# A two-block network on one Trainium2 core: where the last gates, a norm, the state tables and a square root stand

## The chip, the cores and the metric

One core of a Trainium2 chip runs the whole program. Its engines work side by side, each through its own list of instructions in order: TensorE (PE; its weight loads are listed apart, as PEld), VectorE (DVE), ScalarE (ACT), GpSimd (POOL) and SyncE (SP), which here only starts DMA transfers. They wait for one another through semaphores. The metric is the time of one execution in microseconds (us); less is better.

## The reference

Input and output are 512 tokens of width 1024, in 32-bit floats.

```python
def first_block(x, ...):
    h = rms_norm(x, g_mix)
    u, gb, gc, q, k, v = split(h @ w_in)
    y_conv = gb * short_conv(gc * u, conv_w)           # causal, width 3, 512 columns
    y_attn = dilated_mixture(q, k, v)                  # 8 heads, three dilated windows
    mix = concat(rms_norm(y_conv, g_conv_out), rms_norm(y_attn, g_attn_out))
    x = x + mix @ w_out
    h = rms_norm(x, g_ffn)
    return x + (silu(h @ w_gate) * (h @ w_up)) @ w_down

def second_block(x, c, ...):
    shift, scale, gate = split(silu(c) @ w_mod + b_mod)
    h = rms_norm(x) * (1 + scale) + shift
    xa, za, q, k, v, zb, qi, ki, wi, ga, gb = split(h @ w_in)
    ya = gelu(s5_mixer(xa, ...))                       # state space model, 32 groups of 16, state 64
    g = ya @ w_glu + b_glu
    ya = (g[:, :512] * sigmoid(g[:, 512:]) * silu(za)) @ w_a_o
    yb = (dsa_mixer(q, k, v, qi, ki, wi) * silu(zb)) @ w_b_o   # attention over 128 selected keys
    x = x + gate * ((sigmoid(ga) * ya + sigmoid(gb) * yb) @ w_out)
    return rms_norm(x) * final_g
```

## The kernel before

**Layout.** Activations lie transposed, features on partitions and 512 tokens along the free side. Weights stream through a ring of three buffers; ScalarE rounds each to a high part `wh` (L97), VectorE makes the rest `wl` (L98), and each product is three matmuls of 128x512 (`mm3`, L193 to L195). A 128-column step of a projection over 1024 features is 24 such matmuls.

**Order.** PE's order is the order in which the code is written. The lists of the other engines are made by a scheduler, which pulls ahead what is written under `high_priority`. Both attentions are loops over 32 steps (4 blocks of queries by 8 heads): a score, its softmax (L258 to L265: minimum, exponential, reciprocal, scaling), three steps later the transposes (L306), later the products with the values (L283). Between them the loop calls a *filler* for a set number of steps, so that PE has projections while a softmax runs.

**The first attention** has `conv()` as its filler, and after it `mix_out(ch, sqc)`, the convolution's half of the output projection. Eight blocks `n` of 128 columns are summed; after block 0 comes the norm (`rms`, which issues L219 on PE and then `rms_of`: L225, L228 and the 12 operations of `rsqrt` on VectorE, L204 to L212: a guess from the bits and three Newton steps), and after block 2 `spread` (L236) brings the 4x128 roots to all partitions through PE. `cl3` is the low part of the last convolution channel (L504). `mix_out(yh, sqa)` does the same for the attention's half.

**The feed-forward part** has `ssm_tables` beside it, a generator that is advanced a step at a time. After setting up exponentials, sines (on POOL, `pi`, `pr`) and coefficients, it makes for each of four chunks `c` of 8 groups three tables in DRAM: `tabs[2]` from `ca`, `tabs[0]` from `bts` (PE transposes of `ba`, L933, copied by ScalarE, L934), and `tabs[1]` from `tt`, the direct terms: a block of zeros in SBUF into which eight DMAs lay shifted pieces of `kk`, and which a ninth stores. `bts` and `tt` share one buffer (tag `io`).

**The second attention** has `gates()` as its filler: eight projections with a SiLU, then `tanhs(range(6))`, six of eight projections whose tanh opens the merge, and then `chunk_out(c)` for c of 0 to 3, with one more projection after chunks 0 and 1. A chunk copies 64 states into `hs` (POOL, L1199), loads `cat` (L1202) and `tt` (L1204) from the tables, and issues eight pairs of matmuls, L1208 and L1209. `cat` and `tt` of all chunks go through two buffers in all, so a chunk's loads start when the chunk before has been multiplied.

**The end.** The output projection is followed by the last norm, in two halves of 256 tokens: `norm(0)` among the last products, `norm(1)` behind them. Each is sum (L1386), `rms_of`, `spread` (L236), product, store.

Of the kernel before, what the change touches and what calls it, by code (L numbers as in the profile page):

```python
# [9 lines left out]
F = mybir.dt.float32  # L10
# [8 lines left out]
S = 512  # L19
# [9 lines left out]
RAW = 3  # L29
WARM = 8  # L30
FILLA = (3.0, 4.0, 5.0, 2.6)
# [3 lines left out]
class K:  # L35
# [185 lines left out]

    def rms_of(self, pool, p, n, tag, room=None):
        toks = p.shape[1] // P
        d = pool.tile([P, 4, P], F, name="spd")[:, :toks]
        self.V.tensor_mul(d, p.rearrange("p (i t) -> p i t", t=P),  # L225
                          self.ident[:, None, :].to_broadcast([P, toks, P]))
        s = pool.tile([P, 4], F, name=tag + "s")[:, :toks]
        self.V.tensor_reduce(s, d, axis=AX.X, op=OP.add)  # L228
        return self.rsqrt(pool, s, 1.0 / n, EPS, tag, room)

# [85 lines left out]
    def mixer(self):  # L316
# [179 lines left out]
        def conv():  # L496
# [43 lines left out]
            for _ in range(3):  # L540
                yield
            yield from mix_out(ch, sqc)

        def mix_out(ys, sq):

            pend = []
            for n in range(8):
                if n % 2 == 0:
                    wh, wl = self.w()
                p = self.acc()  # L550
                cs = slice(n % 2 * P, n % 2 * P + P)
                yield from self.steps(p, (wh[:, :, cs], wl[:, :, cs]), ys)
                with self.tc.high_priority(offset=LEAD):
                    if n == 0:
                        r = self.rms(sm, [sq], 512, "rx")
                    if n == 2:
                        Rn = self.spread(sm, r, sm.tile([P, S], F, name="Rx"))
# [20 lines left out]
        self.drain()  # L578
        self.run(mix_out(yh, sqa))
        cst.close()  # L580
# [4 lines left out]
    def ffn(self, x1):  # L585
# [10 lines left out]
        tabs = ExitStack()  # L596
        table = self.ssm_tables(tabs)
        for _ in range(2):
# [221 lines left out]

    def ssm_tables(self, st):
        nc, a, V, A, G, T = self.nc, self.a, self.V, self.A, self.G, self.T
# [51 lines left out]
        yield  # L874
        nr = p.tile([P, 48], F, name="snr")
        V.tensor_scalar(nr, pr[:, 1], -1.0, None, op0=OP.add)
# [27 lines left out]
        yield  # L904
        self.tabs = self.dram.tile([3, 4, P, S * 2], F, name="tabs")
        for c in range(4):
            gs = slice(8 * c, 8 * c + 8)
            def table(x, y, nj, name):
# [17 lines left out]
                                ca[:, :, 1:].rearrange("p g j x -> p g (j x)"))  # L926
            bts = p.tile([P, 8, P], F, name="bts", tag="io")
            kk = p.tile([16, 8, P], F, name="kk")
# [20 lines left out]
            V.tensor_add(kk[:, :, 0:16], kk[:, :, 0:16], de)  # L949
            tt = p.tile([P, 8, P], F, name="tt", tag="io")  # L950
            G.memset(tt, 0.0)
            for j in range(8):
                s = 7 - j
                nc.sync.dma_start(tt[16 * j:16 * j + 16, :, 16 * s:], kk[:, :, 0:P - 16 * s])
            nc.sync.dma_start(self.tabs[1, c], tt.rearrange("p g x -> p (g x)"))

# [57 lines left out]
    def hybrid(self, xs, second, close, out):  # L1014
# [222 lines left out]
        def gates():  # L1237
# [8 lines left out]

            yield from tanhs(range(6))
            for _ in cin:
# [3 lines left out]
            for c in range(4):  # L1252
                yield from chunk_out(sso, c)
                yield from tanhs(range(6 + c, min(7 + c, 8)))

# [77 lines left out]
        for m in range(4):  # L1333
# [6 lines left out]
            for e in range(2):  # L1340
# [6 lines left out]
                mg.append((hi, lo))  # L1347
        sq = x3p.tile([P, S], F, name="sqE")
        ws = [self.w() for _ in range(2)]
        ps = [self.acc() for _ in range(2)]  # L1350
# [27 lines left out]
        def norm(e):  # L1378
# [6 lines left out]
            with self.tc.high_priority(offset=200):  # L1385
                T.matmul(p, self.ones, sqs[e][3], start=False, stop=True)  # L1386
                r = self.rms_of(x3p, p, D, "re")
            for k in range(8):
# [15 lines left out]
        self.run(last(5, 1))  # L1404
        self.pad(x3p, 352)
        first, second = norm(0), norm(1)
# [110 lines left out]
```

## Time and profile before

| what | value |
|---|---|
| three runs, us | 1020.39, 1019.31, 1023.4 (median 1020.39) |
| profiled execution, us | 1019.43 |
| its span in the trace, us | 1017.6 |
| PE busy, us (share of the span) | 992.5 (98%) |
| DVE busy, us | 687.6 (68%) |
| ACT busy, us | 420.7 (41%) |
| POOL busy, us | 145.2 (14%) |
| mean granted clock of TensorE, share of full speed | 0.994 |

The span is the time from the first to the last instruction of the trace; the profiled execution's own time is 1.83 us longer. The two clocks of TensorE's matmuls are 2.4 GHz (a granted clock of 1.00) and 1.2 GHz (0.50). Lines are those of the kernel before; in the changed kernel the same code stands 15 lines lower behind `rms_of`, and up to 31 lower towards the end.

### The profile page before, as it was taken

To read this page: it belongs to the slowest core of one execution; us is meant where nothing else is said; L and a number is where in the kernel's file an instruction comes from. 1 tells how busy PE (TensorE), PEld (TensorE's weight loads), DVE (VectorE), ACT (ScalarE), POOL (GpSimd) and SP (SyncE) were. 2 spreads that over 40 slices of the span, in tenths; PEclk is the share of its full clock that TensorE was granted. 3 is DMA by queue.
4 is the path that set the end of the run, shared out by engine and by line. 5 is a ranking of instruction groups with operands and counts; after the bars stand their busy time and mean duration, and the time that the engine had idled before them with its cause. 6 is when DMAs were issued, how large, how long until landed. Compare 5 with 4: busy or idle time off the path is not lost.

```text
span 1017.6 us, 13862 instructions
## 1 busy us (share of the span) xinstructions
PE 992.5 (98%) x5074; PEld 824.4 (81%) x5074; DVE 687.6 (68%) x1334; ACT 420.7 (41%) x710; POOL 145.2 (14%) x324
## 2 busy tenths in 40 slices
PE   9999999999999999999999999999999979999995
PEld 7888887887777778888888898788888878888885
DVE  6886778786997847787653238599995555544444
ACT  6455556443333333233222225556445553333251
POOL 0000000007711100000010100001888130000020
PEclk9999999999999999999999999999999999999998
DMA  7343221223245576465552323343222352343212
GB/s 268 98 135 104 79 84 42 63 89 127 67 142 171 142 219 213 144 203 185 169 170 90 114 93 129 121 133 112 89 83 104 109 160 63 116 173 104 83 42 83
DMA packets 56100, 125.12 MB, mean 123 GB/s; under 512 B 17824, under 2 KB 24480, under 8 KB 55904
## 3 DMA queue, kind: packets, MB, share of 16 engines
q1 hardware_dynamic: 55888, 124.19, 37.6%
q8 instruction: 40, 0.66, 0.3%
q14 instruction: 28, 0.23, 0.1%
q10 hardware_dynamic: 144, 0.05, 0.0%
HBM read 110.45 MB, written 12.58 MB: 121 GB/s over the span
## 4 chain that ended last, share of the span: by engine, by line
PE 89%; DVE 3%; DMA 3%; POOL 3%; issue 1%; SPq 1%; ACT 0%; DVEq 0%; ACTq 0%; POOLq 0%
PE acc L193 24%; PE acc L195 23%; PE acc L194 23%; PE acc L376 2%; PE acc L374 2%; PE acc L375 2%; PE acc L283 2%; PE tp L306 2%; PE sc L255 1%; PE sc L254 1%; DVE wl L98 1%; POOL stt L751 1%; PE acc L1209 1%; PE acc L1152 1%; PE acc L1208 1%
## 5 line engine op out<-in xcount | busy, mean ns | idle before, releaser
L97 ACT CAST wh<-raw 128x1024 fp32r<-128x1024 f32 x156 | 161.6, 1037 | 300.0 <-PE acc L194 245.9
L98 DVE TENSOR_TENSOR wl<-raw,wh 128x1024 fp32r<-128x1024 f32 x156 | 188.8, 1211 | 92.8 <-ACT wh L97 91.3
L193 PE MATMUL acc<-fh,wh 128*128 128x512 f32 x336 | 133.1, 396 | 2.2 <-DVE gs L617 2.2
L195 PE MATMUL acc<-fh,wl 128*128 128x512 f32 x336 | 131.1, 390 | 0.0
L194 PE MATMUL acc<-fl,wh 128*128 128x512 f32 x336 | 131.0, 390 | 0.0
L193 PE MATMUL acc<-hh,wh 128*128 128x512 f32 (+1 forms) x280 | 111.7, 399 | 0.0
L195 PE MATMUL acc<-hh,wl 128*128 128x512 f32 (+1 forms) x280 | 109.6, 391 | 0.0
L194 PE MATMUL acc<-hl,wh 128*128 128x512 f32 (+1 forms) x280 | 109.4, 391 | 0.0
L193 PEld LDWEIGHTS acc<-fh,wh 128*128 128x128 f32 x336 | 63.1, 188 | 17.1 <-DVE gs L617 2.6
L195 PEld LDWEIGHTS acc<-fh,wl 128*128 128x128 f32 x336 | 63.1, 188 | 13.3
L193 PE MATMUL acc<-th,wh 128*128 128x512 f32 (+1 forms) x198 | 73.7, 372 | 0.0
L194 PEld LDWEIGHTS acc<-fl,wh 128*128 128x128 f32 x336 | 63.2, 188 | 12.9 <-issue 0.2
L195 PE MATMUL acc<-th,wl 128*128 128x512 f32 (+1 forms) x198 | 73.4, 371 | 0.0
L194 PE MATMUL acc<-tl,wh 128*128 128x512 f32 (+1 forms) x198 | 73.4, 371 | 0.0
L195 PEld LDWEIGHTS acc<-hh,wl 128*128 128x128 f32 (+1 forms) x280 | 52.2, 186 | 12.1
L262 ACT ACTIVATE e<-z,mn 128x128 f32<-128x128 f32 (+3 forms) x64 | 36.1, 564 | 61.0 <-DVE mn L258 60.8
L193 PEld LDWEIGHTS acc<-hh,wh 128*128 128x128 f32 (+1 forms) x280 | 52.3, 187 | 10.5 <-issue 1.2
L194 PEld LDWEIGHTS acc<-hl,wh 128*128 128x128 f32 (+1 forms) x280 | 52.3, 187 | 9.6
L1162 POOL TENSOR_TENSOR hm<-H,a 128x64 f32<-128x64 f32 x63 | 28.0, 444 | 116.0 <-ACT H L1156 111.1
L193 PEld LDWEIGHTS acc<-th,wh 128*128 128x128 f32 x198 | 37.3, 189 | 7.1
L194 PEld LDWEIGHTS acc<-tl,wh 128*128 128x128 f32 x198 | 37.3, 188 | 7.1
L195 PEld LDWEIGHTS acc<-th,wl 128*128 128x128 f32 x198 | 37.3, 188 | 7.0
(400 smaller groups left out, 2080.6 us busy)
## 6 DMA issues: line engine op xcount, KB each, us to landing
raw<-in_wgu SPq DMA_DIRECT2D x44, 512.0 KB, 3.6
raw<-in_win SPq DMA_DIRECT2D x37, 512.0 KB, 3.5
mraw<-in_wmod SPq DMA_DIRECT2D x24, 512.0 KB, 4.6
raw<-in_wout SPq DMA_DIRECT2D x16, 512.0 KB, 3.5
raw<-in_wdown SPq DMA_DIRECT2D x16, 512.0 KB, 3.5
raw<-in_wconv SPq DMA_DIRECT2D x12, 512.0 KB, 3.5
raw<-in_wqkv SPq DMA_DIRECT2D x10, 512.0 KB, 4.2
x<-in_xT SPq DMA_DIRECT2D x16, 256.0 KB, 5.0
```

What stands on the lines that cost most here:

```text
L97: self.A.copy(hi, raw)
L98: self.V.tensor_sub(lo, raw, hi.bitcast(F))
L193: self.T.matmul(out, lh, rh, start=start, stop=False)
L194: self.T.matmul(out, lh, rl, start=False, stop=False)
L195: self.T.matmul(out, ll, rh, start=False, stop=stop)
L262: self.A.activation(e[:, :n], z[:, :n], AF.Exp, bias=mn, scale=-1.0, accum_out=den)
L283: self.T.matmul(self.yp[64 * e:64 * e + 64, pr * P:(pr + 1) * P], value(j, 2 * pr + e), pTs[u - h0 + 2 * pr + e][:, j * P:(j + 1) * P], st ...
L306: self.T.transpose(pp[:, j * P:(j + 1) * P], e[:, j * P:(j + 1) * P], self.ident)
L374: T.matmul(ps[i], xh[k][:, t], wh[:, kk], start=k == 0, stop=False)
L375: T.matmul(ps[i], xh[k][:, t], wl[:, kk], start=False, stop=False)
L376: T.matmul(ps[i], xl[k][:, t], wh[:, kk], start=False, stop=k == 7)
L1162: G.tensor_mul(m, H[:, c - 1, None].to_broadcast([P, 2, 2, 16]), self.a8.rearrange("p (w r) g -> p w r g", w=2))
```

## The change

It has five parts, each in another place of the program.

1. **Gates.** `tanhs(range(5))` instead of `range(6)` ahead of the chunks, and one projection after each of chunks 0, 1 and 2.
2. **`mix_out`.** Blocks 0 and 1 share a weight and are now interleaved: three of four steps of block 0, three of block 1, then the fourth of each. The norm is issued after block 1's three steps for the convolution (`late` of 1), after block 0's three for the attention (`late` of 0).
3. **Tables.** `nr` (the sines' follower) lives in a rotating `gs` buffer of the feed-forward part. `bts` gets a buffer of its own. `tt` in SBUF, its clearing by POOL and its store are gone: four stores put zeros into the tables in DRAM (896 pieces of 448 bytes each), and the eight pieces of `kk` (rows of 64 to 512 bytes) are stored straight over them. A chunk has one more step.
4. **Root.** The last norm takes a square root on ScalarE, a reciprocal and one Newton step (6 operations) instead of `rsqrt` (12); one root of a single column is computed ahead of the output projection.
5. **Warm-up.** Ten matmuls of ones at the start instead of eight.

```diff
-WARM = 8
+WARM = 10
...
+    def root(self, pool, s, scale, eps):
+        sh = list(s.shape)
+        v, t, y = (pool.tile(sh, F, name="root" + c) for c in "vty")
+        V = self.V
+        V.tensor_scalar(v, s, scale, eps, op0=OP.mult, op1=OP.add)
+        self.A.activation(t, v, AF.Sqrt)
+        V.reciprocal(y, t)
+        V.scalar_tensor_tensor(v, v, -0.5, y, op0=OP.mult, op1=OP.mult)
+        V.tensor_mul(t, v, y)
+        V.scalar_tensor_tensor(y, t, 1.5, y, op0=OP.add, op1=OP.mult)
+        return y
...
-        def mix_out(ys, sq):
+        def mix_out(ys, sq, late):
...
+                if n == 0:
+                    p, p1 = self.acc(), self.acc()
+                    c1 = slice(P, 2 * P)
+                    for e, (q, c) in enumerate(((p, cs), (p1, c1))):
+                        yield from self.steps(q, (wh[:, :, c], wl[:, :, c]), ys, range(3))
+                        if e == late:
+                            with self.tc.high_priority(offset=LEAD):
+                                r = self.rms(sm, [sq], 512, "rx")
+                    yield from self.steps(p, (wh[:, :, cs], wl[:, :, cs]), ys, range(3, 4))
+                elif n == 1:
+                    p = p1
+                    yield from self.steps(p, (wh[:, :, cs], wl[:, :, cs]), ys, range(3, 4))
...
                 with self.tc.high_priority(offset=LEAD):
-                    if n == 0:
-                        r = self.rms(sm, [sq], 512, "rx")
                     if n == 2:
                         Rn = self.spread(sm, r, sm.tile([P, S], F, name="Rx"))
...
-        nr = p.tile([P, 48], F, name="snr")
+        nr = room()
...
+        zt = p.tile([P, 112], F, name="zt")
+        G.memset(zt, 0.0)
...
-            bts = p.tile([P, 8, P], F, name="bts", tag="io")
+            yield
+            tt = self.tabs[1, c].rearrange("p (g x) -> p g x", g=8)
+            nc.sync.dma_start(tt[0:112, :, 0:112], zt[0:112, None].to_broadcast([112, 8, 112]))
+            bts = p.tile([P, 8, P], F, name="bts")
...
-            tt = p.tile([P, 8, P], F, name="tt", tag="io")
-            G.memset(tt, 0.0)
             for j in range(8):
                 s = 7 - j
                 nc.sync.dma_start(tt[16 * j:16 * j + 16, :, 16 * s:], kk[:, :, 0:P - 16 * s])
-            nc.sync.dma_start(self.tabs[1, c], tt.rearrange("p g x -> p (g x)"))
...
-            yield from tanhs(range(6))
+            yield from tanhs(range(5))
...
-                yield from tanhs(range(6 + c, min(7 + c, 8)))
+                yield from tanhs(range(5 + c, min(6 + c, 8)))
...
+        one = x3p.tile([P, 1], F, name="one")
+        A.activation(one, self.ones[:, 0:1], AF.Sqrt)
...
-                r = self.rms_of(x3p, p, D, "re")
+                r = self.rms_of(x3p, p, D, "re", root=True)
...
-        self.pad(x3p, 352)
+        self.pad(x3p, 320)
```

**PE, the joint between chunks 2 and 3 in the second attention.** `acc` is a sum in PSUM, `hh0` to `hh7` and `hl0` to `hl7` are the two parts of the block's input, `e` a softmax. Before, the last pair of chunk 2, then chunk 3's first pair, then the products with the values:

```order
L1208 MATMUL acc_8187<-hs_8177,cat_8183 128x64
L1209 MATMUL acc_8187<-U_5776,tt_8185 128x64
L1208 MATMUL acc_8250<-hs_8240,cat_8246 128x64
L1209 MATMUL acc_8250<-U_5776,tt_8248 128x64
L283 MATMUL acc_8134<-pT_8151,vt_5912 64x128
```

In the changed kernel (the 18 rows of `hh2` to `hh7` are left out):

```order
L1237 MATMUL acc_8120<-hs_8110,cat_8116 128x64
L1238 MATMUL acc_8120<-U_5772,tt_8118 128x64
L193 MATMUL acc_8190<-hh0_4616,wh_7872 128x512
L194 MATMUL acc_8190<-hl0_4617,wh_7872 128x512
L195 MATMUL acc_8190<-hh0_4616,wl_7873 128x512
L321 MATMUL tp_8200<-ident_88,e_8079 128x128 x4
L321 MATMUL tp_8205<-ident_88,e_8103 128x128 x4
L193 MATMUL acc_8190<-hh1_4618,wh_7872 128x512
...
L195 MATMUL acc_8190<-hh7_4630,wl_7873 128x512
L1237 MATMUL acc_8246<-hs_8236,cat_8242 128x64
L1238 MATMUL acc_8246<-U_5772,tt_8244 128x64
L298 MATMUL acc_8133<-pT_8150,vt_5908 64x128
```

A whole projection, 24 matmuls, and two groups of transposes now stand between the chunks.

**VectorE, the end of the convolution's norm.** `rxv`, `rxt` and `rxy` are the variables of `rsqrt`; L258 with `sc_1968` and `sc_1970` is the minimum over the score that PE has issued right ahead of the spread of `rxy`. Before:

```order
L212 SCALAR_TENSOR_TENSOR rxv_1853<-rxt_1854,rxv_1853 128x4
L209 TENSOR_TENSOR rxt_1854<-rxv_1853,rxy_1855 128x4
L210 SCALAR_TENSOR_TENSOR rxy_1855<-rxt_1854,rxy_1855 128x4
L491 TENSOR_REDUCE sqy_821<-s2y_1895 128x128
...
L265 TENSOR_SCALAR e_1942<-e_1942,rd_1945 128x512
L258 ISA z_1971,mn_1972<-sc_1968,lc_103 128x512
L258 ISA mn_1972 128x1
```

In the changed kernel:

```order
L280 TENSOR_SCALAR e_1944<-e_1944,rd_1947 128x512
L210 SCALAR_TENSOR_TENSOR rxy_1894<-rxt_1893,rxy_1894 128x4
L212 SCALAR_TENSOR_TENSOR rxv_1892<-rxt_1893,rxv_1892 128x4
L273 ISA z_1973,mn_1974<-sc_1970,lc_105 128x512
L273 ISA mn_1974 128x1
L209 TENSOR_TENSOR rxt_1893<-rxv_1892,rxy_1894 128x4
L210 SCALAR_TENSOR_TENSOR rxy_1894<-rxt_1893,rxy_1894 128x4
L279 RECIPROCAL rd_1979<-den_1977 128x1
```

The norm's last two operations have moved from eleven rows ahead of that minimum to right behind it. On PE the spread stands where it stood, behind the same score (L255, now L270).

**ScalarE, the merge and the last norm of the changed kernel.** `ACT_TABLE_LOAD` brings in the table of a set of functions; the kernel before has one, at its start. `one` is the root of a single column, `th` a tanh, `roott` the root of the norm.

```order
L1379 ACT_TABLE_LOAD
L1379 ACTIVATE one_9084<-ones_71 128x1
L1344 ACTIVATE yah3_8625<-th_8606 128x512
L97 CAST wh_8680<-raw_8678 128x1024
L1366 ACT_TABLE_LOAD
L1366 ACTIVATE th_8643<-acc_8644 128x512
...
L1420 ACTIVATE x3_8634<-x3_8634,cols_86 128x256
L228 ACT_TABLE_LOAD
L228 ACTIVATE roott_9388<-rootv_9387 128x2
L1406 ACTIVATE s2_9429<-x3_8634 128x256
...
L228 ACTIVATE roott_9485<-rootv_9484 128x2
```

The early root stands ahead of the last tanhs, so the tables change three times, the third time right ahead of the first half's root; the second half's root has none ahead of it.

## Rows read from the trace of the kernel before

**Rows 1.** The page: busy time of each engine (share of the span), instructions.
```profile
PE 992.5 (98%) x5074; PEld 824.4 (81%) x5074; DVE 687.6 (68%) x1334; ACT 420.7 (41%) x710; POOL 145.2 (14%) x324
```
**Rows 2.** Waits of PE, whole span: us in total, times, longest.
```profile
PE acc L1208 <- DMA cat<-tabs: 5.5, 1, 5.5
PE tp L236 <- DVE rey L210: 4.0, 3, 3.2
...
PE tp L933 <- ACT bts L934: 1.7, 1, 1.7
...
PE acc L194 <- DVE cl L504: 0.8, 1, 0.8
...
PE tp L940 <- DVE ca L920: 0.5, 1, 0.5
```
**Rows 3.** Timeline of PE, 822 to 845 us: start, duration, instruction, [idle before].
```profile
822.61 1.97 PE L283 MATMUL acc<-pT,vt 128*64 128x128 f32 x32
...
833.52 0.39 PE L1209 MATMUL acc<-U,tt 128*128 128x64 f32 x2
839.38 0.66 PE L1208 MATMUL acc<-hs,cat 128*128 128x64 f32 x2 [5.47 <-DMA cat<-tabs]
...
841.12 3.50 PE L283 MATMUL acc<-pT,vt 128*64 128x128 f32 x32
844.55 0.44 PE L1208 MATMUL acc<-hs,cat 128*128 128x64 f32 x2
```
**Rows 4.** Windows there: stretch, length, PE, PEld, DVE, ACT, POOL, clock, DMA share, GB/s.
```profile
839.30:843.00 3.70, 3.16 (x22) 2.89 (x24) 0.00 (x0) 0.00 (x0) 0.00 (x0) 0.50 0.30 75
```
**Rows 5.** Tile view of `cat` (two rows), then line view of L1204 (`tt`).
```profile
L1208 PE MATMUL acc<-hs,cat x64: 217/275/447, 801.6 to 847.4; 128*128 128x64 f32 x64
...
DMA to landing us min/median/max: 3.5/4.3/5.5
...
DMA to landing us min/median/max: 4.3/5.1/6.4
```
**Rows 6.** Timeline of POOL: the copies of chunk 0's states.
```profile
786.13 3.78 POOL L1199 COPY hs<-H 64x252 f32<-64x252 f32 x4
```
**Rows 7.** Timeline of the last norm: VectorE, PE (both halves), ScalarE.
```profile
1008.52 0.17 DVE L204 TENSOR_SCALAR rev<-res 128x2 f32<-128x2 f32 x1
...
1010.45 0.16 DVE L210 SCALAR_TENSOR_TENSOR rey<-ret,rey 128x2 f32<-128x2 f32 x1
...
1001.70 0.71 PE L236 MATMUL tp<-ident,rey 128*128 128x128 f32 x4 [0.39 <-DVE rey L210]
...
997.34 0.51 ACT L1389 ACTIVATE x<-x,cols 128x256 f32<-128x256 f32 x1
```
**Rows 8.** Timeline of the start, ScalarE and PE.
```profile
1.17 1.28 ACT L64 ACT_TABLE_LOAD   x1 [1.17 <-PEq L1507]
2.46 0.20 ACT L64 ACTIVATE warm<-ones 128x1 f32<-128x1 f32 x1
...
0.99 3.77 PE L67 MATMUL tp<-ones 128*128 128x128 f32 x16 [0.99 <-POOL ones L62]
...
6.21 0.50 PE L376 MATMUL acc<-wh,xl 128*128 128x512 f32 x1
```
**Rows 9.** Timeline of PE and VectorE around the convolution's spread.
```profile
179.15 0.39 PE L255 MATMUL sc<-kT,qT 128*128 128x512 f32 x1
179.38 0.83 PE L236 MATMUL tp<-ident,rxy 128*128 128x128 f32 x6
...
179.73 0.68 DVE L258 CUSTOM_DVE_ANT_0 z<-sc,lc 128x512 f32<-128x512 f32 x1
```
**Rows 10.** Timeline of ScalarE at chunk 0's tables.
```profile
321.84 0.58 ACT L934 COPY bts<-tp 128x512 f32<-128x512 f32 x1 [5.32 <-DMA tabs<-tt]
```
**Rows 11.** Windows at 235 us; SP; line view of L1220, stores of 256-byte pieces.
```profile
235.00:240.00 5.00, 5.00 (x24) 4.14 (x23) 1.97 (x4) 0.85 (x1) 4.45 (x12) 1.00 0.00 0
...
241.49 0.34 SPq L119 DMA_DIRECT2D raw<-in_wgu  x1
...
DMA to landing us min/median/max: 1.6/1.7/3.7
```

More of the change, by code (lines that the diff above doesn't have):

```diff
@@ L220, in rms, with rms_of @@
         return self.rms_of(pool, p, n, tag, room)
-    def rms_of(self, pool, p, n, tag, room=None):
+    def root(self, pool, s, scale, eps):
[9 more added lines that the diff above has]
+        return y
+    def rms_of(self, pool, p, n, tag, room=None, root=False):
         toks = p.shape[1] // P
@@ L228, in rms_of @@
         self.V.tensor_reduce(s, d, axis=AX.X, op=OP.add)
+        if root:
+            return self.root(pool, s, 1.0 / n, EPS)
         return self.rsqrt(pool, s, 1.0 / n, EPS, tag, room)
@@ L541, in conv @@
                 yield
-            yield from mix_out(ch, sqc)
-        def mix_out(ys, sq):
+            yield from mix_out(ch, sqc, 1)
+        def mix_out(ys, sq, late):
             pend = []
@@ L549, in mix_out @@
                     wh, wl = self.w()
-                p = self.acc()
                 cs = slice(n % 2 * P, n % 2 * P + P)
-                yield from self.steps(p, (wh[:, :, cs], wl[:, :, cs]), ys)
+                if n == 0:
[10 more added lines that the diff above has]
+                    yield from self.steps(p, (wh[:, :, cs], wl[:, :, cs]), ys, range(3, 4))
+                else:
+                    p = self.acc()
+                    yield from self.steps(p, (wh[:, :, cs], wl[:, :, cs]), ys)
                 with self.tc.high_priority(offset=LEAD):
-                    if n == 0:
-                        r = self.rms(sm, [sq], 512, "rx")
                     if n == 2:
@@ L578, in mixer @@
         self.drain()
-        self.run(mix_out(yh, sqa))
+        self.run(mix_out(yh, sqa, 0))
         cst.close()
@@ L596, in ffn @@
         tabs = ExitStack()
-        table = self.ssm_tables(tabs)
+        table = self.ssm_tables(tabs, lambda: wg.tile([P, S], F, name="gs", bufs=2)[:, :48])
         for _ in range(2):
@@ L819, in sincos, with ssm_tables @@
         return out
-    def ssm_tables(self, st):
+    def ssm_tables(self, st, room):
         nc, a, V, A, G, T = self.nc, self.a, self.V, self.A, self.G, self.T
```

## The prediction

> **What bounds the kernel now.** I read the page's busy times first: TensorE is at work for 992.5 of 1017.6 us [rows 1], and the parts of the change take or add only a few matmuls. So it can win only where PE stands still, 25 us in all. PE's list of waits says where [rows 2]; five of its lines lie in the places that the change touches: 5.5 for `cat`, 4.0 for the root of the last norm, 1.7 for `bts`, 0.8 for `cl`, 0.5 for `ca`. Then I read the timeline at each.
>
> The `cat` wait costs more than its line says. The last pair of chunk 2 ends at 833.91; chunk 3's first pair starts at 839.38, after 5.47 idle, and the 32 products with the values behind it take 3.50 us, where the same group took 1.97 before the stop [rows 3]. The windows show why: the granted clock is 0.50, the 1.2 GHz level, from 839.3 to 843 [rows 4]. The chunks' work goes on at full pace at 844.55.
>
> **Part 1, gates.** From 833.91 to 844.55 are 10.64 us. Work done in them: one pair of chunk matmuls (0.22 each at their quickest [rows 5], so 0.45) and 32 value products (1.97 at full clock [rows 3]), 2.42 in sum. The rest, 8.2 us, is the stop and its slow clock. In the changed order 24 projection matmuls and two groups of transposes stand in the joint: 24 x 0.23 (one 512-column matmul starts that long before the next [rows 9]) + some 0.9 (six 128-column ones took 0.83 [rows 9]) = 6.4 us; the joints after chunks 0 and 1 hold, counted likewise, about 7.5. The projection isn't added work, only moved. The loads start when the last pair has been read. `cat` landed at most 5.5 us after its issue and `tt` at most 6.4, issued 0.4 later [rows 5]. Against 6.4 us of cover `cat` is in time, and `tt` can be late by 0 to 0.6. Chunk 0 now comes a projection earlier, at about 793 to 796 instead of 801.6 [rows 5]; its states are copied by 789.91 [rows 6], so that cover, 3 us at least, holds. I take -8.0; bounds -8.5 and -6 (a late `tt` and another short stretch at the low clock).
>
> **Part 2, mix_out.** The interleaving puts three more steps ahead of the step that waits for `cl3`; nine matmuls at 0.23 cover 0.77. But the norm is issued later, and its last two operations now stand behind the minimum over the score that PE issues right ahead of the spread. Before, PE went from that score (179.15) to the spread (179.38) without a stop, and VectorE took the minimum from 179.73 to 180.41 [rows 9]. Now PE must wait for that minimum and for two small operations, which in the last norm start 0.2 us apart [rows 7]: 180.41 + some 0.1 for reading out + 0.4 + 0.14 to release PE is 181.0, against 179.38: 1.6. VectorE has more queued there than before, so I take 1.8. No other work of PE can pass, since its order is fixed. The exchange: -0.77 + 1.8 = +1.0. Bounds: -0.8, if VectorE gets to the norm earlier than its place suggests, and +1.7.
>
> **Part 3, tables.** ScalarE's copy into `bts` waited 5.32 us for the store of `tt`, since the two shared a buffer [rows 10]; PE felt 1.67 of it. With a buffer of its own the wait has no cause: -1.66. With `nr` in another place VectorE reaches `ca` earlier by about 1 us, more than the wait of 0.46: -0.46 [rows 2]. POOL loses four clearings of `tt`. Four zero stores are new, 1.6 MB in 3584 pieces; on SyncE they stand behind the parameter loads, ahead of the weight load that started at 241.49. From 235 to 240 the DMA engines moved nothing [rows 11], so I cost them at nothing; if they aren't done by then, they delay weights (a rival, below). What the small stores of `kk` take is not in this trace; the nearest rows are stores in 256-byte pieces to DRAM, 1.6 to 3.7 us to landing [rows 11], and the first chunk that reads a table comes at 801.6 [rows 5], long after. I take -2.1; bounds -2.4 and -1.0 (half of the wait comes back elsewhere).
>
> One rule speaks against this part. The rows just named show 32 KB in 256-byte pieces landing in 1.7 us in the middle. The Trainium skill, "DMA: Bandwidth & Descriptors" (the table at its top), gives 512 bytes as the least transfer for line rate, with a read-modify-write below it. By that the zeros, at 448 bytes, would take longer than their bytes say; the sum would stay as it is as long as they end before the next weight load.
>
> **Part 4, root.** Behind the sum of the second half, VectorE's 12 operations run from 1008.52 to 1010.61, 2.09 us [rows 7]. Six replace them: 0.17 for the first, a root on ScalarE of about 0.20 (the one small ACTIVATE right behind a table load [rows 8]), four at 0.2, and two crossings between engines, some 0.14 less or more each: 1.25. So -0.85 on the path, of the 4.0 us of waits. The first half's 0.39 [rows 7] goes too if the root's table is there in time. It isn't loaded by the early root, since the tanhs behind that bring theirs back. But the third load waits for nothing: ScalarE is free from 997.85 [rows 7], 1.28 us [rows 8] more are 999.13, and the root and what follows it end near 1000.3; PE came to the spread at 1001.31, so a microsecond is left. I take -0.85 - 0.35 = -1.2; bounds -1.4 and -0.5. The two loads in the merge fall into times in which ScalarE waits for PE; the cover there is about 11 us, and without it they would cost 1.3 each.
>
> The trace's only load took 1.28 us, and the next operation of ScalarE began 0.01 behind it [rows 8]. The Trainium skill, "ScalarE: Activation LUTs" (What ACT_TABLE_LOAD costs), puts 1.38 us of drain on top, 2.66 per change of set. By that the root would start at 1000.5 and the first half would keep a wait of some 0.4: -0.85 for this part instead of -1.2, and 1010.4 for the sum.
>
> **Part 5, warm-up.** Eight matmuls of ones take 3.77 us [rows 8], so two more end at 5.70 instead of 4.76. That pushes the first two real matmuls by a quarter of a microsecond, but the third waited until 6.21 for `xl` [rows 8]. 0; bounds -0.2 and +0.3.
>
> **Sum.** -8.0 + 1.0 - 2.1 - 1.2 + 0 = -10.3 against the profiled execution's 1019.43: 1009.1. The median of the three runs lies 0.96 above that execution; so I say 1010.1. All lower bounds together would give 1007.1, all upper ones 1014.9.
>
> **Rivals.**
> *No new wait at the spread.* Against it is the order of VectorE; for it, that VectorE may be ahead of PE there. Part 2 then gives -0.8 and the time is 1008.3.
> *The joints don't hold.* The landing times come from four loads of each kind at other moments; if one is a microsecond later at the narrowest joint, or if a chunk ahead of a score delays a softmax, PE stops for 1 to 2 us in one or two joints, and with a slow clock behind each, 2 to 5 us come back: 1012 to 1015.
> *The early root doesn't do what it is there for*, since its table is thrown out; if the third load also starts late, at the sum, 1.3 us lie on the first half's path, of which 0.4 shows, and the time is 1010.5 to 1011.
> *Slower.* The mechanism is the zero stores in the queue ahead of the weights. If 128 pieces take 1.7 us (32 KB of 256 bytes [rows 11]) and don't overlap, 3584 take 48 us. Issued a little before 230, they would end at about 277, and the weight load of 241.49 would come 36 us late. Weights are split about two half blocks ahead of PE, 2 x 24 x 0.23 = 11 us; so PE would stand for 25 us, and the time would be 1035. PE feels it from 23 us for all the zeros on; 33 us eat the whole gain, and from 38 the change is slower by over 0.5%. Against it: sixteen engines share the pieces, and the row is a time to landing, much of it the same for any size.
>
> **Chances.** The forecast as summed, with its smaller doubts: 0.58. No new wait: 0.15. Joints: 0.16. A late third load: 0.06. Zero stores that delay weights: 0.05. A measurement of this kernel tells about 0.5%, 5.1 us, from no change, so faster means below 1015.3. Within 0.5% fall the worst joints (0.03), zeros that cost some 5 to 15 us (0.02), and the forecast's own case where most upper bounds come together (0.04): 0.09. Slower are the zeros alone, 0.03. That leaves 0.88 for faster. The range leaves out those 0.12 at the top, with 0.02 just below the bound, and some 0.05 at the bottom, where no wait forms at the spread, the rest comes at its lower bounds and the runs scatter downwards: 1006.5 to 1014.5.
>
> **What would show it.** In the trace after: no stop of PE at the chunks, and a granted clock near 1.00 from 800 to 850 (part 1 wrong if a wait for `cat` or `tt` of over 1 us stands there). A wait of PE for `rxy` of 1.5 to 2 us at about 179 instead of the one for `cl` (part 2 wrong if neither or both are there). No wait for `bts` or `ca`, and weights that land when they did (part 3). About 2.3 us instead of 3.2 ahead of the last spread, and three table loads with PE waiting for none (part 4). The forecast is wrong if the stop at the chunks only moves to another joint, or if weights come late at 245 to 280.

## The result, and the profile after

The changed kernel takes 1010.66 us (median of four runs, 1009.39 to 1012.38), the kernel before 1020.27 beside it: a ratio of 0.9897, 95% interval 0.9871 to 0.9923. So it is faster by 1.0%, and clear of the 0.5% that a measurement tells. The profiled execution took 1009.39 us, its span is 1007.6.

The page's first row and PE's list of waits, of the changed kernel (us in total, times, longest):

```profile
PE 990.9 (98%) x5078; PEld 823.2 (82%) x5078; DVE 683.1 (68%) x1320; ACT 426.1 (42%) x716; POOL 137.7 (14%) x321
```

```profile
PE tp L251 <- DVE rooty L232: 2.3, 1, 2.3
PE acc L193 <- DVE gs L643: 2.2, 1, 2.2
PE tp L251 <- DVE rxy L210: 1.4, 1, 1.4
PE tp L1417 <- ACT s L1406: 1.0, 1, 1.0
...
PE tp L321 <- DVE e L280: 1.0, 1, 1.0
PE tp L251 <- DVE rfy L210: 0.8, 1, 0.8
```

Of the five waits of [rows 2], those for `cat`, `bts`, `cl` and `ca` are gone and the one for the last root is down from 3.2 to 2.3. New are `rxy` (1.4), which the prediction named, and `e` (1.0), which it didn't.

The timeline of PE at the joint between chunks 2 and 3, and a window over it (columns as in [rows 4]):

```profile
826.67 0.39 PE L1238 MATMUL acc<-U,tt 128*128 128x64 f32 x2
...
833.31 0.33 PE L1237 MATMUL acc<-hs,cat 128*128 128x64 f32 x2
833.47 0.39 PE L1238 MATMUL acc<-U,tt 128*128 128x64 f32 x2
```

```profile
826.00:834.00 8.00, 8.00 (x50) 6.91 (x51) 3.15 (x4) 4.55 (x7) 2.83 (x6) 1.00 0.61 229
```

Where [rows 3] show a stop of 5.47 us and a slow stretch behind it, PE works without a gap and the granted clock stays 1.00. From the last pair of one chunk to the first of the next are 6.6 us, filled by a projection.

To see where the rest went I set the same matmuls of the traces side by side and took the time between landmarks of PE. A stretch runs from the start of one such matmul to the start of the next. The table is worked out from the timelines (us); "low" says that the first matmuls behind the wait for `gs`, a wait of some 2.2 us that ends at 262 to 265, ran at the low clock, granted 0.50:

| stretch of PE | before | changed | E1 | E2 | E3 | E4 | E5 |
|---|---|---|---|---|---|---|---|
| start to first score | 76.69 | 76.82 | 78.41 | 77.00 | 77.22 | 76.87 | 76.87 |
| first attention, to the score behind the spread of `rxy` (part 2) | 103.50 | 105.05 | 103.47 | 103.50 | 104.98 | 104.98 | 105.04 |
| to the next norm's spread (`rfy`) | 72.78 | 73.07 | 72.33 | 73.90 | 72.12 | 73.59 | 73.85 |
| to the end of the feed-forward part (part 3) | 357.02 | 354.52 | 356.43 | 356.13 | 356.35 | 356.10 | 354.52 |
| low clock behind `gs` there | no | no | no | low | low | low | no |
| second attention, chunks (part 1) | 55.22 | 46.85 | 47.25 | 46.85 | 46.85 | 46.86 | 46.86 |
| merge, to the last norm | 148.55 | 148.54 | 148.54 | 148.54 | 148.54 | 148.54 | 148.54 |
| first half's norm (part 4) | 10.62 | 9.95 | 10.61 | 9.95 | 9.95 | 10.61 | 9.94 |
| second half's norm (part 4) | 3.88 | 2.98 | 3.88 | 2.99 | 2.99 | 3.89 | 2.99 |
| last spread to the end | 6.85 | 7.30 | 7.39 | 7.35 | 7.50 | 7.08 | 7.11 |

The stretch between the feed-forward part and the chunks (182.5 us in every run) is left out. Changed against before, the column adds up to the 10.0 us between the spans: -8.37 chunks, -2.50 feed-forward part, -0.67 and -0.90 last norm; +1.55 first attention, +0.29 next norm, +0.13 start, +0.45 end.

### The profile page after: what moved, and what is told of

Its sections match the earlier page's. It is cut to its first block, busy times and chain, and to the rows that moved or that the text cites. A ratio compares the mean times of both kernels' runs of the same rounds, so it can differ in the third digit from the quotient of the medians.

```text
span 1007.6 us, 13842 instructions
## 1 busy us (share of the span) xinstructions
PE 990.9 (98%) x5078; PEld 823.2 (82%) x5078; DVE 683.1 (68%) x1320; ACT 426.1 (42%) x716; POOL 137.7 (14%) x321
## 4 chain that ended last, share of the span: by engine, by line
PE 93%; DVE 2%; POOL 2%; DMA 1%; issue 1%; ACT 1%; SPq 0%; DVEq 0%; POOLq 0%
PE acc L193 25%; PE acc L195 24%; PE acc L194 24%; PE acc L389 2%; PE acc L391 2%; PE acc L390 2%; PE acc L298 2%; PE tp L321 2%; PE sc L270 1%; PE sc L269 1%; DMA sg<-in_sgn 1%; PE acc L1237 1%; POOL stt L777 1%; PE acc L1238 1%; PE acc L1181 1%
```

## The experiments

Each was timed beside the kernel before on the same chip; the ratio is to that kernel. Since starts and low clocks differ from execution to execution by 1 to 2 us, verdicts on single parts rest on the stretches. Most repeat to 0.1 us; the next norm (72.1 to 73.9 over all runs), the start and the end do not, and the feed-forward part takes 1.6 more where the clock falls.

### E1: the gates alone

The kernel before with only

```diff
-            yield from tanhs(range(6))
+            yield from tanhs(range(5))
-                yield from tanhs(range(6 + c, min(7 + c, 8)))
+                yield from tanhs(range(5 + c, min(6 + c, 8)))
```

> The kernel before with part 1 alone (five gates ahead, one behind each of three chunks). Theory: the stop for `cat` and the low clock behind it are the whole of part 1, and nothing of the other parts is needed. Then no wait for `cat` or `tt` stands in PE's list, the first product of the merge starts 8.4 us earlier than before (at 839.3 instead of 847.7), the other waits stay, and the span is 1009.2. Rival: the joints hold in the changed kernel only because its other parts shift the loads; then a wait for `cat` or `tt` of 1 us or more remains, with a stretch at the low clock, and the gain is under 6 us.

1012.66 us, ratio 0.9931 (0.9908 to 0.9955). The chunks' stretch fell from 55.22 to 47.25, 7.97 us. PE's list:

```profile
PE tp L236 <- DVE rey L210: 4.0, 3, 3.2
...
PE tp L933 <- ACT bts L934: 1.2, 1, 1.2
...
PE acc L194 <- DVE cl L504: 0.8, 1, 0.8
...
PE tp L940 <- DVE ca L920: 0.5, 1, 0.5
PE acc L1209 <- DMA tt<-tabs: 0.2, 1, 0.2
```

The stop for `cat` is gone without any other part; a `tt` was late by 0.2, and the stretch is 0.4 longer than in the changed kernel. The expected span of 1009.2 was missed by 1.6, since this execution began 1.7 us slower. The theory holds: part 1 stands by itself.

### E2: `mix_out` undone

The changed kernel with `mix_out` of the kernel before.

> The changed kernel with `mix_out` as before. Theory: part 2 costs 1.6 us in the first attention and 0.3 more at the next norm (its spread waits 0.77 instead of 0.50), since its waits only moved. Then the wait for `cl` of 0.77 is back, the waits for `e` (0.97) and `rxy` (1.43) are gone, the feed-forward part's wait for `gs` ends at 261.9 instead of 263.75, and the span is 1005.8. Rival: part 2 gains and the delay comes from the warm-up or from the zero stores; then the wait for `gs` ends at 263.7 or later and the span is 1007.6 or more.

1008.51 us, ratio 0.9898 (0.9874 to 0.9922). The first attention took 103.50 again instead of 105.05: part 2 costs 1.55 us there. The 0.29 of the next norm didn't come back; the wait for `rfy` was 1.6 here. And the feed-forward part took 1.6 longer than in the changed kernel, though its code is the same: the eight matmuls behind the wait for `gs` ran at the low clock. So the span was 1008.7 where 1005.8 was expected. The wait for `gs` ended at 263.24, between the 261.9 of the theory and the 263.7 of the rival. So the theory holds for the first attention and not for the span, and something was at work that neither had: the low clock.

### E3: the tables undone

The changed kernel with `ssm_tables` of the kernel before: `nr` of its own, `bts` and `tt` in one buffer, no zero stores.

> The changed kernel with the tables as before (`nr` of its own, `tt` in SBUF, one buffer for `bts` and `tt`). Theory: part 3 gains 2.5 us between the feed-forward part's first wait for `gs` and its end. Then the waits for `bts` (1.7) and `ca` (0.5) are back and the span is 1010.1. Rival: those waits went because VectorE and PE stand 2 us later against each other there; then they don't come back in full and the span is 1007.6 to 1008.5.

1010.6 us, ratio 0.9917 (0.9894 to 0.994), span 1009.0. ScalarE's copy waits as it did in [rows 10], but PE waits neither for `bts` nor for `ca`. The timeline of ScalarE, that of PE 60 us earlier, and the window there:

```profile
322.64 0.59 ACT L960 COPY bts<-tp 128x512 f32<-128x512 f32 x1 [4.72 <-DMA tabs<-tt]
```

```profile
263.12 0.80 PE L193 MATMUL acc<-fh,wh 128*128 128x512 f32 x1 [2.23 <-DVE gs L643]
263.71 0.63 PE L194 MATMUL acc<-fl,wh 128*128 128x512 f32 x1
...
266.27 0.48 PE L194 MATMUL acc<-fl,wh 128*128 128x512 f32 x1
266.59 0.39 PE L195 MATMUL acc<-fh,wl 128*128 128x512 f32 x1
```

```profile
263.20:266.00 2.80, 2.80 (x7) 2.22 (x8) 2.80 (x7) 0.74 (x2) 2.49 (x8) 0.50 0.00 0
```

Here the clock fell to its lower level behind the wait for `gs`, and PE lost 1.6 us in eight matmuls. That made it late, and later than the tables. With the low clock the part took 356.35 with the old tables (E3) and 356.10 to 356.13 with the new ones (E2, E4); without it 356.43 and 357.02 (E1, before) and 354.52 (changed, E5). So part 3 is worth 1.9 to 2.5 us where the clock holds and 0.2 where it falls. The theory of 2.5 always falls. The rival is right that the waits don't come back, but the span of 1009.0 lies outside its range too, and its reason does not fit: PE waits 2.2 for `gs` with the late first attention and without it, so the two engines stand the same against each other from there. That is argued; the old tables with the late first attention and a clock that holds are in no profile. By the medians this run is no slower than the changed kernel (1010.66, and 1010.51 in E5), so the whole of part 3 does not show in the time of these executions. Its three pieces were undone together only.

### E4: the root undone

The changed kernel with `rsqrt` in the last norm, the padding of 352, and no early root.

> The changed kernel with `rsqrt` in the last norm, without the early root, and with the padding of before. Theory: the root gains 0.65 us in the first half's norm and 0.9 in the second's, and gives 0.5 back where the granted clock falls ahead of the last spread. Then PE waits 3.2 ahead of the last spread, that spread takes 0.7 instead of 1.2, and the span is 1008.7. Rival: the low clock there isn't tied to the root and comes here too; then the spread takes 1.2 and the span is 1009.1.

1012.75 us, ratio 0.9935 (0.9914 to 0.9956). The two halves' norms took 10.61 and 3.89, as before: the root gives 0.66 and 0.91, 1.57 in sum. The span of 1011.0 is above both expectations, since the clock fell behind `gs` (1.6) and the next norm took 0.5 longer than in the first profile. The last spread took 1.2 here too, so its slow clock isn't the root's; the rival holds on that point. The clock need not fall there either: in the kernel before, and with the root in E7, that spread took 0.68 behind stops of 3.19 and 2.29.

### E5: the changed kernel again

> The changed kernel once more, as the control of this call and for what its executions differ by. Theory: the place of every wait is fixed, but whether the granted clock falls behind a stop of some 2 us is chance: in three of six profiles seen so far (all with a wait for `gs` of 2.2) about eight matmuls behind that wait run at the low clock and cost 1.6 us, and the last spread takes 0.7 or 1.2. So its span lies between 1007 and 1010.5, and the differences to the first profile of it stand at these places and at the start alone. Rival: the same program repeats to 0.3 us, and the differences between the runs so far are of their edits.

1010.51 us, ratio 0.9902 (0.9885 to 0.9918), span 1008.2. Every stretch with a part of the change in it repeated to 0.01 us. What differed stood at the end, as expected, and at one place that the theory hadn't: the wait for `rfy` was 1.6 instead of 0.8. The clock held behind `gs` in this one. In all profiles together the wait for `gs` of 2.2 to 2.7 stands eleven times, and five times the clock fell behind it (E2, E3, E4, E6, E8).

### E6: the norm in the stop

The convolution's norm is issued a step of block 1 earlier, ahead of the transposes that wait for `e`:

```diff
-                        yield from self.steps(q, (wh[:, :, c], wl[:, :, c]), ys, range(3))
+                        yield from self.steps(q, (wh[:, :, c], wl[:, :, c]), ys, range(1) if late and e else range(3))
                         if e == late:
+                            if late:
+                                self.mm3(q, wh[:, 1, c], wl[:, 1, c], ys[1][0], ys[1][1], False, False)
                             with self.tc.high_priority(offset=LEAD):
                                 r = self.rms(sm, [sq], 512, "rx")
+                    if late:
+                        yield
+                        yield from self.steps(p1, (wh[:, :, c1], wl[:, :, c1]), ys, range(2, 3))
```

> The changed kernel with the convolution's norm issued one step of block 1 earlier, right ahead of the transposes that wait for `e`. Theory: in part 2 the wait for `cl` became one for `e` (0.97), and the late norm made one for `rxy` (1.43); a norm issued in the first stop costs PE nothing there and is done in time for the spread. Then the wait for `rxy` is gone, `e` is at most 0.5, and the score behind the spread starts 1.7 to 2.5 us earlier than in the changed kernel (at 179.5 to 180.2 instead of 181.87); the span is 1.7 to 2.8 shorter. Rival: VectorE is the bound in this stretch, and the earlier norm pushes softmaxes back; then PE waits as long for `e` or for sums elsewhere, and the score starts within 0.5 us of 181.87.

1008.82 us, ratio 0.9881 (0.9862 to 0.99), beside 1010.51 for the changed kernel in E5. The score behind the spread started at 180.12 instead of 181.87, and the stretch took 103.44, a little less than before the change. PE's list:

```profile
PE tp L321 <- DVE spd L238: 0.6, 1, 0.6
...
PE tp L219 <- DVE sqc L528: 0.2, 1, 0.2
```

The waits for `e` and `rxy` are gone but for these. The theory holds; the span was only 0.4 shorter, since the clock fell behind `gs`.

### E7: two products on GpSimd

```diff
-        V.tensor_mul(w, pi[:, 1], ai)
+        G.tensor_mul(w, pi[:, 1], ai)
-        V.tensor_mul(ci, pi[:, 1], ar)
+        G.tensor_mul(ci, pi[:, 1], ar)
```

> The changed kernel with two products of the tables (with `pi`, 128x48) on GpSimd instead of VectorE. Theory: the wait of 2.2 for `gs` at 261 to 264 is VectorE standing behind these two, which wait for `pi`, while the sums that it could free are ready. Then that wait is gone or under 0.5, the low clock behind it too, and the part up to its end at 609 is 2.2 to 3.8 us shorter. Rival: VectorE, full in the next 30 us, gives it back as waits for sums or tables; then it is shorter by under 1 us.

1009.99 us, ratio 0.9892 (0.9874 to 0.991). The wait for `gs` is gone, and with it the place where the clock fell; but the part took 354.25 instead of 354.52. PE's list:

```profile
PE tp L972 <- ACT kk L975: 0.8, 1, 0.8
PE tp L972 <- DVE ca L949: 0.6, 1, 0.6
...
PE acc L195 <- DVE wl L98: 0.3, 1, 0.3
```

What PE won at 263 it waited for at the tables. The rival holds: against an execution whose clock stays up it gives 0.3, against one whose clock falls 1.9.

### E8: the zeros twice

```diff
             nc.sync.dma_start(tt[0:112, :, 0:112], zt[0:112, None].to_broadcast([112, 8, 112]))
+            nc.sync.dma_start(tt[0:112, :, 0:112], zt[0:112, None].to_broadcast([112, 8, 112]))
```

> The changed kernel with each of the four zero stores issued twice (3.2 MB instead of 1.6). Theory, by the prediction: PE feels the zeros when they take over 23 us; once they took about 16 (231 to 247), so twice they take some 32, and PE waits 5 to 10 us for weights between 250 and 275; the span is 1013 to 1018. Rival: weights pass between the pieces, as they did in the changed kernel (a weight load was issued at 243.2, before the last zeros landed), and PE waits under 1 us for them.

1010.92 us, ratio 0.9903 (0.9876 to 0.9929), no different from E5. A window with the DMA engines full (the last three columns: granted clock, DMA share, GB/s), and ScalarE's wait for the next weight:

```profile
240.00:245.00 5.00, 5.00 (x21) 3.77 (x21) 3.77 (x5) 2.95 (x3) 4.41 (x8) 1.00 1.04 286
```

```profile
249.43 1.05 ACT L97 CAST wh<-raw 128x1024 fp32r<-128x1024 f32 x1 [5.78 <-DMA raw<-in_wgu]
```

No wait of PE for a weight stands in its list; the one for `gs` is 2.7 instead of 2.2, and the feed-forward part took 356.58, 0.45 more than in the other runs whose clock fell there with the new tables (356.10 to 356.14). The last of the second stores was issued at 245.2 and landed at the latest 7.1 us later: 3.2 MB took some 20 us, not 32. The rival holds, within its 1 us. Its remark on the changed kernel, and the 16 us of the theory, do not: there the zeros had ended before the weight load of 243.2, 12 us after the first was issued (the lines stand under part 3 below). How many zeros it takes until PE waits for a weight was not reached.

### E9: the zeros late

```diff
-        G.memset(zt, 0.0)
+        G.tensor_scalar(zt, pi.rearrange("p a b -> p (a b)")[:, 320:432], 0.0, None, op0=OP.mult)
```

> The changed kernel with the zeros made from the last powers of the tables (times nought), so that their four stores go out some 40 us later, between the weight loads of the feed-forward part. Theory: the early stores do cost something: the parameters `bc` and `sg`, loaded right ahead of them, land 8.2 to 9.2 us after their issue instead of 6.3 to 7.7, VectorE waits 4.2 instead of 2.6 for `sg`, GpSimd's chain for `pi` stands behind it for 1.8, and the next norm's spread waits 0.8 to 1.6 instead of 0.5 or less. Then `sg` lands in under 7.8 us, the wait for `rfy` is at most 0.5, and from the score behind the convolution's spread to that spread are at most 72.4 us instead of 73.1 to 73.9; if the later stores harm nothing, the time is about 1 us shorter. Rival: those differences are chance, or the later stores delay weights; then no shorter.

1010.18 us, ratio 0.9894 (0.9879 to 0.9909). The timelines of VectorE and GpSimd, of E5 and then of E9:

```profile
239.32 0.49 DVE L930 TENSOR_SCALAR bc<-bc,sg 128x512 f32<-128x512 f32 x1 [4.22 <-DMA sg<-in_sgn]
239.94 0.82 POOL L944 COPY ca<-bc 128x128 f32<-128x128 f32 x1 [1.77 <-DVE bc L930]
```

```profile
238.09 0.48 DVE L930 TENSOR_SCALAR bc<-bc,sg 128x512 f32<-128x512 f32 x1 [3.09 <-DMA sg<-in_sgn]
238.70 0.82 POOL L944 COPY ca<-bc 128x128 f32<-128x128 f32 x1 [0.64 <-DVE bc L930]
```

`sg` came a microsecond earlier and GpSimd's chain with it, and the wait for `rfy` was 0.5. But `sg` still took 7.9 us to land, the stretch to the spread took 72.8 where at most 72.4 was expected, and in E10, with the zeros early, it took 72.36. The time is no shorter beyond the intervals. The other profiles help: in the eight with early zeros `sg` landed 7.6 to 9.0 us after its issue (mean 8.4) and the stretch to that spread took 73.16 on average; in the six without (the kernel before, E1, E3, E9, E11 and E12) 6.3 to 7.9 (mean 7.2) and 72.47. So the zeros delay the parameters by about 1 us, and the stretch is 0.7 longer in the mean; but not each time, since its shortest value of all, 72.11, is that of E8 with the zeros twice.

### E10: the last stop filled, no early root

```diff
-        one = x3p.tile([P, 1], F, name="one")
-        A.activation(one, self.ones[:, 0:1], AF.Sqrt)
...
+            if e == 1:
+                d = self.tp()
+                for _ in range(8):
+                    T.matmul(d[:, :P], self.ones, self.ones, start=True, stop=True)
             with self.tc.high_priority(offset=200):
                 Rl = self.spread(x3p, r)
```

> The changed kernel with eight matmuls of ones, whose result nothing reads, in PE's last stop, and without the early root of one column. Theory: the low clock ahead of the last spread comes from the stop alone and falls by chance inside it or not (the spread took 0.7 or 1.2, with the root and without it); with PE at work the spread takes 0.7, and the end comes 0.4 to 0.5 us earlier after the last sum. The early root does nothing: its table is thrown out by the tanhs behind it, so without it one table load is left in the stretch, at the same place, and no wait of PE moves. Rival: the matmuls delay the spread, or the third load, now the only change of set, comes late and the first half's spread waits.

1011.21 us, ratio 0.9901 (0.9885 to 0.9917). The last spread in the timeline of the changed kernel and the window that holds it, then the same two in E10:

```profile
1000.30 1.19 PE L251 MATMUL tp<-ident,rooty 128*128 128x128 f32 x4 [2.29 <-DVE rooty L232]
```

```profile
1000.00:1002.00 2.00, 1.19 (x4) 0.93 (x4) 0.62 (x3) 0.00 (x0) 0.00 (x0) 0.50 0.00 0
```

```profile
997.61 1.95 PE L1423 MATMUL tp<-ones 128*128 128x128 f32 x16
1000.06 0.68 PE L251 MATMUL tp<-ident,rooty 128*128 128x128 f32 x4 [0.50 <-DVE rooty L232]
```

```profile
1000.00:1002.00 2.00, 0.68 (x4) 0.52 (x4) 1.22 (x4) 0.00 (x0) 0.00 (x0) 1.00 0.00 0
```

With PE at work the clock stayed up and the spread took 0.68; VectorE began the product that follows 3.70 us behind the last sum instead of 4.21. The end did not follow: it came 10.12 us behind that sum, against 10.28 in the first profile and 10.10 in E5, so the expected 0.4 to 0.5 were not gained, and the median is no shorter. No wait moved for want of the early root. But the merge took 148.97 instead of 148.54: without a single new wait, the 512-column matmuls from 950 to 975 us started 0.233 us apart instead of 0.227.

### E11 and E12: the four edits together

E11 is the changed kernel with the edits of E6, E7, E9 and E10. E12 keeps the early root's column in its place, filled with ones by GpSimd:

```diff
-        A.activation(one, self.ones[:, 0:1], AF.Sqrt)
+        G.memset(one, 1.0)
```

> The changed kernel with the four edits together: the convolution's norm in the first stop, the two products with `pi` on GpSimd, the zeros late, and the last stop filled without the early root. Theory: they lie in different places and their gains add: 1.75 (norm), 1 (zeros), 0.3 to 1.8 (products: the wait for `gs` and the low clock behind it), 0.5 (end): 3.5 to 5 us, a time of about 1006. Rival: VectorE is the bound from 263 to 300 us, and what comes earlier there waits for it; then only the norm's and the end's part is left, 2.2 us, 1008.3.

> The kernel of all four edits, with the place of the early root's column kept in memory (filled with ones by GpSimd, no root). Theory: in the two runs without that column the 512-column products of the output projection, 950 to 975 us, started 0.233 us apart instead of 0.227, and the 256-column ones behind them a little closer, 0.4 us more in sum; nothing but the place of the later buffers, 32 bytes lower, had changed there. Then the pace is 0.227 again, from the first product of the merge to the first sum are 148.5 us instead of 149.0, and the time is 0.4 us below that of the run before, about 0.9865 of the kernel before. Rival: the pace goes with the missing table loads or by chance; then it stays 0.233, or comes and goes, and the time is as before.

E11: 1007.75 us, ratio 0.9869 (0.9852 to 0.9887). E12: 1006.56 us, ratio 0.9862 (0.9832 to 0.9892). E12's stretches: 103.43 in the first attention, 72.33, 354.24, 46.85 in the chunks, 148.54, 9.95 and 2.99. PE's list in E12:

```profile
PE tp L1422 <- ACT s L1411: 1.0, 1, 1.0
PE tp L67 <- POOL ones L62: 1.0, 1, 1.0
PE tp L977 <- ACT kk L980: 0.9, 1, 0.9
PE tp L977 <- DVE ca L954: 0.6, 1, 0.6
...
PE tp L251 <- DVE rooty L232: 0.5, 1, 0.5
```

No wait is over 1.0 us, and the mean granted clock is 0.999. The 0.42 of the merge came back with the column (148.54 against 148.96 in E11), so the pace went with the column's place in memory. The rival of the missing table loads falls with E4 as well: it has neither column nor root and one table load, but 32 bytes more of padding, and its merge took 148.54. E11's time lies between the 1006 of its theory and the 1008.3 of the rival, and neither holds in full. Against the first profile of the changed kernel the norm gave 1.66, the next norm 0.6 and the tables 0.2, the merge took 0.42 back and the start 0.8, so the span is 1.3 shorter. The price of the low clock behind `gs` can be won only against executions in which it falls. E12's expectation holds. It is the fastest version here, 4.1 us below the changed kernel by the medians and 2.7 by the profiled spans. The intervals of E11 and E12 end below the changed kernel's ratio of 0.9897 but overlap its interval; no single execution of the two was as slow as the fastest of the changed kernel.

## Why the prediction was right

Forecast 1010.1 us, measured 1010.66. Most of it came as worked out, and some of the agreement is luck: parts 1, 3 and 4 gave 1.1 us more than forecast in the first profile, part 2 and three places outside the sum (next norm, start, end) cost 1.4 more. The step from the profiled execution to the median, 0.96 in the sum, was 1.27.

**Part 1** was forecast at -8.0 and gave 8.37 in the changed kernel, 7.97 alone (E1). The reading that the low clock behind the stop belongs to its price carried this: the wait's own line said 5.5. The allowance for a late `tt` of 0 to 0.6 came out at 0 to 0.4 by PE's lists and 0 to 0.6 by the stretch, which was 47.48 in E7.

**Part 2** was forecast at +1.0 and cost 1.55 (E2). The wait for `rxy` came where the order of VectorE put it, for the 1.8 that I took: 1.43 in the list, and 1.6 by the spread's start, which came 1.82 behind the score's instead of 0.23. VectorE's and PE's timelines:

```profile
180.48 0.16 DVE L209 TENSOR_TENSOR rxt<-rxv,rxy 128x4 f32<-128x4 f32 x1
180.67 0.16 DVE L210 SCALAR_TENSOR_TENSOR rxy<-rxt,rxy 128x4 f32<-128x4 f32 x1
...
180.98 1.13 PE L251 MATMUL tp<-ident,rxy 128*128 128x128 f32 x8 [1.43 <-DVE rxy L210]
```

The step that failed is "nine matmuls at 0.23 cover 0.77", as a gain of 0.77. They did cover `cl`; but PE, no longer stopped there and with the norm's matmul moved behind it, came earlier to the transposes of `e`, which VectorE finished no sooner, and waited 0.97. I followed the wait to its removal and not to who is late next.

**Part 3** was forecast at -2.1 and gave 2.50 in the first profile. Its size is not a constant, as E3 shows: where the clock falls behind the wait for `gs`, PE is late anyway and the part gives 0.2. "So I cost them at nothing", of the zeros, was right for the weights, and for the reason given. The four stores were issued from 231.2 to 238.1, and when SyncE started the next weight load the DMA engines had just come to rest (windows of the changed kernel, columns as in [rows 4], then SyncE's timeline):

```profile
242.00:243.00 1.00, 1.00 (x5) 0.57 (x3) 1.00 (x1) 1.00 (x2) 0.96 (x1) 1.00 0.11 32
243.00:244.00 1.00, 1.00 (x5) 0.75 (x4) 1.00 (x2) 0.80 (x1) 0.92 (x2) 1.00 0.00 0
...
243.19 0.36 SPq L119 DMA_DIRECT2D raw<-in_wgu  x1
```

The rival's price, 48 us for all zeros, was four times too high, for they were through in 12: a store of 32 KB took 1.7 us to land [rows 11], one of the zeros, 392 KB, 5.0 to 8.8, so much of that row's time does not grow with the bytes, as the prediction allowed. The pieces of 448 bytes moved a little more slowly than weights: from 240 to 241 the zeros made 277 GB/s at a DMA share of 1.01, from 244 to 248 the weight loads of the kernel before 260 at 0.79, so by the engines' busy time a sixth less. The zeros' small cost, parameters about 1 us later and some 0.7 in the next norm's stretch (E9), wasn't in the sum.

**Part 4** was forecast at -1.2 and gave 1.57 (E4): 0.9 in the second half for 0.85, 0.66 in the first for 0.35, since the wait costs more than its 0.39: without it the spread also overlaps the matmul ahead of it (some 0.17) and takes 0.1 less itself. The early root's table was thrown out as the order shows, and the third load was hidden. ScalarE's timeline in the changed kernel:

```profile
988.98 1.28 ACT L228 ACT_TABLE_LOAD   x1
990.27 0.20 ACT L228 ACTIVATE roott<-rootv 128x2 f32<-128x2 f32 x1
```

The root began 0.01 us behind the load. The Trainium skill, "ScalarE: Activation LUTs" (What ACT_TABLE_LOAD costs), adds 1.38 us of drain to each change of set; this load, right behind another operation of ScalarE and right ahead of the root, shows none, and the first half's spread did not wait.

**Part 5** was forecast at 0; the start was 0.13 later in the first profile, less than what starts differ by (76.67 to 78.41 over all runs), so it stays unmeasured.

**Not in the sum** was the end: the last spread took 1.19 instead of 0.68, since the clock had already fallen in the stop ahead of it. E4 (no root, 1.2) and E7 (root, 0.68) show that this isn't the root's, and E10 to E12 that with work in the stop the clock stayed up, three times of three.

## What to carry to other kernels

A stop of the engine that sets the time can cost more than its line says, by a slow stretch behind it, so read the granted clock there; work that is moved into the stop from elsewhere can win both. Where a wait is taken away, go on along that engine's order to the next instruction that another engine feeds: here that one was late by more (0.97 for 0.77). And compare stretches between fixed instructions of two traces, not spans: parts of 0.5 us show there to a few hundredths where the clock holds, while executions of one program differ by 1 to 2 us.

## What the runs showed of the hardware

The clock may or may not fall behind a stop of some 2 us: behind the same wait for `gs` (2.2 to 2.7 us) it fell in five of eleven profiles, 1.0 to 0.50 for about eight matmuls, and cost 1.6 us. These are ten programs, with the same code around the wait; that chance decides is the simplest reading, and the mean granted clock of one program's executions differs too (E2: 0.994 to 0.997). With eight matmuls of ones in the last stop, the spread behind it ran at full pace in all three runs that had them (E10 to E12); without them it did so in two of eleven (the kernel before and E7).

The pace of matmuls with nothing waiting went from 0.227 to 0.233 us for 512 columns when a column was left out ahead of other buffers, and back when its place was kept (E10 to E12). It was 0.227 too in E4, where the column is left out but the padding behind it is 32 bytes larger (352 for 320). Which buffer's address does it, and why, the runs don't tell. Part of the timeline of PE in E11, then in the changed kernel:

```profile
960.90 0.39 PE L195 MATMUL acc<-mh,wl 128*128 128x512 f32 x1
961.13 0.40 PE L193 MATMUL acc<-mh,wh 128*128 128x512 f32 x1
961.36 0.39 PE L194 MATMUL acc<-ml,wh 128*128 128x512 f32 x1
961.60 0.40 PE L195 MATMUL acc<-mh,wl 128*128 128x512 f32 x1
```

```profile
960.92 0.39 PE L195 MATMUL acc<-mh,wl 128*128 128x512 f32 x1
961.15 0.39 PE L193 MATMUL acc<-mh,wh 128*128 128x512 f32 x1
961.38 0.39 PE L194 MATMUL acc<-ml,wh 128*128 128x512 f32 x1
961.60 0.39 PE L195 MATMUL acc<-mh,wl 128*128 128x512 f32 x1
```
